# The second norm of a hybrid DiT trunk in two steps: first what feature tile 0 reads, for both groups of tokens, then the rest

## The chip, the cores and the metric

The kernel runs on one NeuronCore of a Trainium2 chip. Its engines are named as in the profile: PE (TensorE, matmuls) with PEld (its weight loads), DVE (VectorE), ACT (ScalarE), POOL (GpSimd) and SP (SyncE, which issues DMAs). The metric is the device time of one execution in microseconds (us), as the median of the runs.

## The reference

Two layers (l = 0, 1) work on 1280 tokens of 1024 features, 256 of context and 1024 of the latent. Each layer norms the tokens, projects them, runs four mixers side by side, projects the result back and adds it to x. Then comes the part that matters here:

```
x  = x + ml[2] * (y @ w_out)
h2 = rmsnorm(x, norm2) * (1 + ml[4]) + ml[3]
u, g = split(h2 @ w_up, 2)
x  = x + ml[5] * ((silu(dwconv(g)) * u) @ w_down)
```

The up-projection has 2 x 2816 columns: 22 feature tiles of 128 for u and as many for g. In layer 1 the context rows are left out.

## The kernel before

Features lie on the partitions and tokens along the free dimension, so an activation is eight tiles k = 0..7 of 128 features. Every matrix product is made of three matmuls on values split into a high part (fp32r) and a low one: hi x hi, hi x lo, lo x hi (`dense_acc`, L312 to L314). `split` (L229, L230) makes the two parts: a cast on ACT, then a subtraction on the engine that is named to it.

**The up-projection.** The latent tokens are two groups of 512: a (256 to 767) and b (768 to 1279). For feature tiles 1 to 21, `ffn_up` takes u and g of both groups at once, as a 2 x 2 block product (u or g columns times low or high features; low features times group a or b) with seven block products in place of eight. That needs combinations of the activations: B11 and B21 (low and high features of group a), T1 (low features of b less those of a), B22 (high features of b) and three more, `tops[2]`, `tops[3]` and `tops[4]`. It needs combinations of the weights too: s12, which POOL makes at L1900 and L1901 into a buffer `wr_s`, and s34, made in place at L1903 and L1904. Feature tile 0 is computed directly. Its first half uses B11 and B21; its second half, into the accumulators `pxu` and `pxg`, uses T1 and B22 alone. The accumulators of the other tiles are `px`, `py`, `pz`, and `pcu` and `pcg` for the context.

The tiles are generators. At the end of `ffn_up` they are run in this order: first half of 0, first half of 1, second half of 0, its convolution (`conv3`, ACT L729, DVE L732 and L733, L1954, L1957), second half of 1, its convolution, then the tiles 2, 3, ... one by one. L1886 loads a tile's weights through SP; L1864 copies an accumulator to the tile `u` or `gp` on ACT, L1867 adds one on DVE.

**The second norm.** Group a is normed early and its scaled values are kept in the tiles `kept` (nk in the profile). Group b comes in two pieces of 256 tokens (768 and 1024). The main program (L1766 to L1776) runs the last part of the output projection, calls `rstd_fast` for each piece (sum of squares, power on POOL, and the row `ro` copied out by ACT at L223), and then `norm_fast` (L258) for the two pieces, one after the other. For each of k = 0..3 `norm_fast` issues eight DVE instructions of 256 columns. L271 scales b12 (feature k) and b22 (feature 4 + k) and is the only one that reads x. L279 makes T1. L280 makes the input of `tops[2]`, L283 that of `tops[3]`, L288 that of `tops[4]`. L287 makes the low part of B22 (ACT makes the high part, L286). One of the splits ends on DVE (`tops[4]`); three end on POOL (T1, `tops[2]`, `tops[3]`). T1 and B22 are written to the tiles hb.

**Buffers.** `norm_fast` takes its temporaries from one tag with three buffers (L268). The pools of x (group b), of `kept` and of these temporaries are closed with `cx`, right behind the calls of `norm_fast`, and the pools w4 and u are opened next:

```
        with pool_(tc, name=f"w4{l}", bufs=3) as wq, pool_(tc, name=f"u{l}", bufs=1) as pool:
            ffn_up(K, l, act, tops, HD, (wp, wq), (ug, pool))
```

`ffn_up` takes raw weight buffers from `wp` (open since before) and `wq` (w4) by turns. The first four (u and g of tiles 0 and 1) are of `wp`; `wr_s` of tile 1 and u and g of tile 2 are of `wq`. The tile `u` of feature tile 1 is of the pool u.

**What sets the order.** The order of each engine's instructions isn't written out. A planner (the tile context, with a timeline simulation) orders them when the program is built, by their place in the source and by when its own costs let them start; a buffer is given out again when the last reader of what lay there is done. On the chip each engine then goes through its queue in that order.

Of the kernel before, what the change touches and what calls it, by code (L numbers as in the profile page):

```python
# [14 lines left out]
OP = mybir.AluOpType  # L15
# [48 lines left out]
def pool_(tc, **kw):  # L64
    return tc.tile_pool(reuse_waits="tile", **kw)


class Kern:
# [188 lines left out]
    def norm_fast(self, l, xs, rb, kept, act, tops, dsh, pool, t0, n):  # L257

        nc = self.nc
        s, d = slice(t0, t0 + n), slice(t0 - LAT[1][0], t0 - LAT[1][0] + n)
        hi, lo = act
        stt = nc.vector.scalar_tensor_tensor

        def temp(name):
            return pool.tile([P, self.nw], F32, tag="ntmp", name=f"{name}{l}1_{t0}", bufs=self.ntmps)[:, :n]

        def scaled(k):
            t = temp(f"nt{k}")  # L270
            stt(t, xs[k], self.ns[l][:, 1, k, 0:1], rb, OP.mult, OP.mult)  # L271
            return t

        for k in range(4):
            sh = self.modv[l][:, 28 + k, 0:1]
            b12, b22 = scaled(k), scaled(4 + k)
            t1, t4 = kept[k][:, d], kept[4 + k][:, d]
            t2 = temp(f"n2{k}")
            nc.vector.tensor_tensor(t1, b12, t1, OP.subtract)  # L279
            stt(t2, b22, sh, t1, OP.add, OP.subtract)  # L280
            self.split(t2, *[v[k][:, d] for v in tops[2]], nc.gpsimd)
            self.split(t1, hi[k][:, s], lo[k][:, s], nc.gpsimd)
            stt(b12, b22, dsh[:, k:k + 1], b12, OP.add, OP.subtract)  # L283
            self.split(b12, *[v[k][:, d] for v in tops[3]], nc.gpsimd)
            h = hi[4 + k][:, s]
            nc.scalar.activation(h, b22, AF.Identity, bias=sh)  # L286
            stt(lo[4 + k][:, s], b22, sh, h.bitcast(F32), OP.add, OP.subtract)  # L287
            stt(t4, t4, sh, t2, OP.add, OP.subtract)  # L288
            self.split(t4, *[v[k][:, d] for v in tops[4]], nc.vector)

# [1189 lines left out]
def trunk(ctx, tc, A, out, dbg=None):  # L1480
    nc = tc.nc
    K = Kern(ctx, tc, A, out, dbg)
# [16 lines left out]
    def open_act(name):  # L1499
        c = ExitStack()  # L1500
        ts = {}
        for q, ks in enumerate(((1, 0), (4, 5, 6, 7), (2, 3))):
            p = c.enter_context(pool_(tc, name=f"h{name}{q}", bufs=1))
            ts.update({(i, k): p.tile([P, T], F32R, name=f"h{name}{i}{k}") for k in ks for i in range(2)})
        return c, [[ts[i, k] for k in range(KT)] for i in range(2)]

    cact = act = None
    for l in range(2):
# [10 lines left out]
        if l == 0:  # L1519
# [3 lines left out]
            cact, act = open_act("a")  # L1523
        with ExitStack() as c1:
# [37 lines left out]
            if l == 0:  # L1562
                with pool_(tc, name="zs", bufs=1) as zp:
                    with pool_(tc, name="np", bufs=1) as npool:

                        xs, rb = {}, {}
# [79 lines left out]
        with ExitStack() as c3:  # L1646
            K.lo_eng = nc.gpsimd
            ep = c3.enter_context(pool_(tc, name=f"ae{l}", bufs=1))
            late = c3.enter_context(pool_(tc, name=f"al{l}", bufs=1))
# [55 lines left out]
        cact, act = open_act(f"b{l}")  # L1705
# [5 lines left out]
        def open_x(stack, order, name, **kw):  # L1711
            return {t0: stack.enter_context(pool_(tc, name=f"{name}{l}{t0}", bufs=1, **kw)).tile([P, KT, n], F32, name=f"{name}{l}{t0}") for t0, n in order}

        def resid(x, part, m):
            def evac(ps, a, n):
                c = 1 if a < TC else 0
                v = xs_(x, a, n)[:, m]
                nc.vector.scalar_tensor_tensor(v, ps, K.modv[l][:, 8 * part + m, c:c + 1], v, OP.mult, OP.add)  # L1718
            return evac

        def xs_(x, t0, n):
            b = max(q for q in x if q <= t0)
            return x[b][:, :, t0 - b:t0 - b + n]

        with ExitStack() as cx:
            x = open_x(cx, groups[-1:], "x")
            kp = cx.enter_context(pool_(tc, name=f"k2{l}", bufs=1))
            dsh = kp.tile([P, 4], F32, name=f"dsh{l}")
            nc.vector.tensor_tensor(dsh, K.modv[l][:, 28:32, 0], K.modv[l][:, 24:28, 0], OP.subtract)
            kept = []  # L1730

            def norm(t0, n, npool):
                r = K.norm_mod(l, 1, [x[t0][:, k] for k in range(KT)], act, t0, n, npool, kp if t0 == TC else None)
                if t0 == TC:
                    kept.extend(r)
                nc.scalar.dma_start(XS[:, :, t0:t0 + n], xs_(x, t0, n))

            with ExitStack() as c1:
                npool = c1.enter_context(pool_(tc, name=f"n2{l}", bufs=1))
                x.update(open_x(c1, groups[-2::-1], "x"))  # L1740
                wo = c1.enter_context(pool_(tc, name=f"wo{l}", bufs=2, side="right"))
                for k in K_ORDER:
                    for t0, n in groups:
                        raw = wo.tile([P, 512], F32, tag="yraw", name=f"yraw{l}_{k}_{t0}", bufs=4)
                        nc.sync.dma_start(raw[:, :n], YD[k][:, t0:t0 + n])
                        K.split(raw[:, :n], act[0][k][:, t0:t0 + n], act[1][k][:, t0:t0 + n], nc.vector if k % 2 else nc.gpsimd)
                    if k == 6:
                        for t0, n in groups:
                            nc.sync.dma_start(x[t0], xd[l][:, :, t0:t0 + n])
                for i, m0 in enumerate(range(0, 8, 2)):  # L1750
                    ms = range(m0, m0 + 2)
                    K.wb = (2, 4) if i % 2 else (1, 2)
                    K.dense_late([A["w_out"][l, m] for m in ms], act, K_ORDER[:-2], K_ORDER[-2:], groups[:-1], [resid(x, 2, m) for m in ms],
                                 wp if i % 2 else wo, [f"out{l}_{m}_{TC}" for m in ms])
                K.wb = (2, 4)
                for q in groups[:-1]:
                    norm(*q, npool)
            npool = cx.enter_context(pool_(tc, name=f"n3{l}", bufs=1))
            K.ntmps, K.nw = 3, 256
            ct = ExitStack()  # L1760
            tops = {q: [ct.enter_context(pool_(tc, name=f"t{q}{l}", bufs=1, side="right")).tile([P, 4, 512], F32R, name=f"top{l}{q}{i}") for i in "hl"] for q in (2, 3, 4)}
            tops = {q: [[v[:, k] for k in range(4)] for v in hl] for q, hl in tops.items()}
            ug = ct.enter_context(pool_(tc, name=f"ug{l}", bufs=1, side="right"))

            for m in range(4):
                K.dense(A["w_out"][l, m], act, KT, LAT[1:], resid(x, 2, m), wp, f"out{l}_{m}_768")  # L1766
            ws = [K.load_w(A["w_out"][l, m], KT, wp, f"out{l}_{m}_768") for m in range(4, 8)]
            late = []
            for t0, n in ((768, 256), (1024, 256)):
                for m, (hi, lo) in zip(range(4, 8), ws):  # L1770
                    ps = K.acc(f"ps_out{l}_{m}_{t0}")[:, :n]
                    K.dense_acc(ps, lambda k: hi[:, k], lambda k: lo[:, k], lambda k: act[0][k][:, t0:t0 + n], lambda k: act[1][k][:, t0:t0 + n], KT)
                    resid(x, 2, m)(ps, t0, n)
                xs = [xs_(x, t0, n)[:, k] for k in range(KT)]
                late.append((xs, K.rstd_fast(l, xs, npool, t0, n), t0, n))
                nc.scalar.dma_start(XS[:, :, t0:t0 + n], xs_(x, t0, n))  # L1776
            for xs, rb, t0, n in late:
                K.norm_fast(l, xs, rb, kept, act, tops, dsh, npool, t0, n)
        K.lo_eng = nc.gpsimd
        K.ntmps, K.nw = 2, 512  # L1780
        with pool_(tc, name=f"w4{l}", bufs=3) as wq, pool_(tc, name=f"u{l}", bufs=1) as pool:
# [32 lines left out]
        with ExitStack() as c3:  # L1814
# [4 lines left out]
            with pool_(tc, name=f"f{l}", bufs=1) as pool:  # L1819
                for i, (b0, b1) in enumerate(((0, 1), (1, 4), (4, 8), (8, 12), (12, 16), (16, 20))):  # L1820
                    with pool_(tc, name=f"e{l}{i}", bufs=1, side="right") as ep:
                        f, n = stages[i] if i < len(stages) else (None, 0)
# [9 lines left out]
            if not last:  # L1832
                cact, act = open_act(f"c{l}")
# [284 lines left out]
```

## Time and profile before

| | us |
|---|---|
| three runs | 3441.28, 3445.07, 3448.4 (median 3445.07) |
| the profiled execution | 3445.22 |
| its span | 3443.4 |
| PE busy | 3191.5 (93%) |
| DVE busy | 2128.9 (62%) |
| ACT busy | 1207.4 (35%) |
| POOL busy | 1177.6 (34%) |

The mean granted clock of TensorE is 0.963 of full speed. Times in the rows are from the start of the span. The second norm and the start of the up-projection lie at about 960 to 1040 us in layer 0 and at 2705 to 2790 us in layer 1. In a timeline a row is: start, duration, engine, line, operation, written tile <- read tiles, shape, count; in brackets how long the engine was idle before, and what released it. Rows of one kind that follow each other are merged, and their duration is that of the whole. Durations of neighbours on DVE, ACT and PE overlap, so the time that one takes in the queue is read from start to start.

### The profile page before, as it was taken

How to read it: one execution, taken by the hardware profiler on the slowest of the kernel's cores; microseconds unless marked ns; L12 is line 12 of the kernel's file. 1: busy time of each engine (PE TensorE's matmuls, PEld its weight loads, DVE VectorE, ACT ScalarE, POOL GpSimd, SP SyncE). 2: the span in 40 equal slices, each digit the busy share in tenths (PEclk: the TensorE clock that was granted, in tenths of full speed). 3: DMA queues.
4: the chain of work that ended last, by engine and by line, in shares of the span. 5: the costliest groups of instructions: out<-in, count | busy, mean ns of one | idle time of the engine just before them, and what ended most of it. 6: DMA issues, size and time to landing. Idle time of an engine off the chain costs nothing. (4 is left out here: it accounts for less than half of the span.)

```text
span 3443.4 us, 47008 instructions
## 1 busy us (share of the span) xinstructions
PE 3191.5 (93%) x17550; PEld 2644.8 (77%) x17550; DVE 2128.9 (62%) x4011; ACT 1207.4 (35%) x2013; POOL 1177.6 (34%) x1109
## 2 busy tenths in 40 slices
PE   7899997998989999998999899997998899999996
PEld 6898995664868888877788789995545788887785
DVE  7758647776484343348788583527755865556645
ACT  4223544334353333342111424533333443434211
POOL 1922424224065444442111011323332475554220
PEclk9999997999999999999999999998999999999998
DMA  5666635247222112126233565533163222223421
GB/s 204 168 198 212 175 104 159 91 145 260 94 75 80 66 66 72 62 96 198 93 104 111 146 179 173 150 114 118 52 227 102 89 92 86 74 92 128 146 68 49
DMA packets 287300, 423.53 MB, mean 123 GB/s; under 512 B 91088, under 2 KB 197344, under 8 KB 287072
## 3 DMA queue, kind: packets, MB, share of 16 engines
q1 hardware_dynamic: 176932, 301.33, 27.9%
q10 hardware_dynamic: 110140, 119.20, 10.4%
q8 instruction: 138, 2.26, 0.3%
q14 instruction: 90, 0.74, 0.1%
HBM read 301.48 MB, written 118.91 MB: 122 GB/s over the span
## 5 line engine op out<-in xcount | busy, mean ns | idle before, releaser
L312 PE MATMUL pd<-fh,wh_d 128*128 128x512 f32 (+1 forms) x896 | 328.8, 377 | 21.9 <-ACT fh L229 12.8
L313 PE MATMUL pd<-fl,wh_d 128*128 128x512 f32 (+1 forms) x896 | 333.1, 375 | 13.3 <-DVE fl L230 13.3
L314 PE MATMUL pd<-fh,wl_d 128*128 128x512 f32 (+1 forms) x896 | 329.1, 372 | 0.0
L230 POOL TENSOR_TENSOR wl_d<-wr_d,wh_d 128x1024 fp32r<-128x1024 f32 x44 | 111.3, 2549 | 467.4 <-ACT wh_d L229 458.1
L1718 DVE SCALAR_TENSOR_TENSOR xx<-pd,modv,xx 128x512 f32<-128x512 f32 (+1 forms) x248 | 164.8, 677 | 118.8 <-PE pd L314 118.4
L312 PE MATMUL ps_in<-ha,wh_in 128*128 128x384 f32 (+3 forms) x688 | 217.0, 325 | 12.0 <-ACT st L1542 11.1
L314 PE MATMUL ps_in<-ha,wl_in 128*128 128x384 f32 (+3 forms) x688 | 222.3, 323 | 0.0
L313 PE MATMUL ps_in<-ha,wh_in 128*128 128x384 f32 (+3 forms) x688 | 222.2, 323 | 0.1
L312 PE MATMUL ps_in<-hc,wh_in 128*128 128x256 f32 (+1 forms) x704 | 214.0, 306 | 5.7 <-ACT hc L244 3.7
L312 PEld LDWEIGHTS pd<-fh,wh_d 128*128 128x128 f32 x896 | 172.3, 194 | 55.5 <-ACT fh L229 15.5
L313 PE MATMUL ps_in<-hc,wh_in 128*128 128x256 f32 (+1 forms) x704 | 213.4, 304 | 0.7 <-DVE hc L245 0.7
L314 PE MATMUL ps_in<-hc,wl_in 128*128 128x256 f32 (+1 forms) x704 | 212.8, 303 | 0.0
L313 PEld LDWEIGHTS pd<-fl,wh_d 128*128 128x128 f32 x896 | 173.1, 194 | 45.5 <-DVE fl L230 18.1
L314 PEld LDWEIGHTS pd<-fh,wl_d 128*128 128x128 f32 x896 | 172.5, 193 | 28.4
L230 POOL TENSOR_TENSOR wlo_u<-wr_u,whi_u 128x1024 fp32r<-128x1024 f32 x44 | 105.7, 2402 | 217.6 <-ACT whi_u L229 195.4
L1040 ACT ACTIVATE a_E<-a_pst 128x1024 f32<-128x1024 f32 (+1 forms) x84 | 84.3, 1003 | 178.7 <-PE a_pst L1038 142.3
L229 ACT CAST wh_d<-wr_d 128x1024 fp32r<-128x1024 f32 x44 | 45.2, 1047 | 289.9 <-PE pd L313 157.2
L312 PEld LDWEIGHTS ps_in<-ha,wh_in 128*128 128x128 f32 x688 | 132.8, 194 | 14.9 <-ACT st L1542 11.8
L230 DVE TENSOR_TENSOR wlo_s<-wr_s,whi_s 128x1024 fp32r<-128x1024 f32 x42 | 70.0, 1667 | 115.3 <-ACT whi_s L229 115.3
L971 DVE TENSOR_REDUCE a_mx<-a_pm 128x1 f32<-128x512 f32 (+1 forms) x192 | 109.2, 595 | 51.3 <-PE a_pm L970 50.6
L312 PEld LDWEIGHTS ps_in<-hc,wh_in 128*128 128x128 f32 x704 | 134.4, 192 | 8.2 <-ACT hc L244 4.8
L313 PEld LDWEIGHTS ps_in<-hc,wh_in 128*128 128x128 f32 x704 | 134.8, 192 | 2.7 <-DVE hc L245 1.9
(648 smaller groups left out, 9437.5 us busy)
## 6 DMA issues: line engine op xcount, KB each, us to landing
wm<-in_w_mod SPq DMA_DIRECT2D x96, 512.0 KB
wr_in<-in_w_in SPq DMA_DIRECT2D x44, 512.0 KB
wr_u<-in_w_up SPq DMA_DIRECT2D x44, 512.0 KB
wr_g<-in_w_up SPq DMA_DIRECT2D x44, 512.0 KB
wr_d<-in_w_down SPq DMA_DIRECT2D x44, 512.0 KB
wr_out<-in_w_out SPq DMA_DIRECT2D x32, 512.0 KB
HD<-u ACTq DMA_DIRECT2D x22, 640.0 KB
hr<-HD SPq DMA_DIRECT2D x22, 640.0 KB
```

What stands on the lines that cost most here:

```text
L229: nc.scalar.copy(hi, src)
L230: (eng or nc.gpsimd).tensor_tensor(lo, src, hi.bitcast(F32), OP.subtract)
L312: mm(ps, whi(k), ahi(k), start=start and i == 0, stop=False)
L313: mm(ps, whi(k), alo(k), start=False, stop=False)
L314: mm(ps, wlo(k), ahi(k), start=False, stop=stop and i == len(ks) - 1)
L971: nc.vector.tensor_reduce(mf[:, c:c + 1] if c < 2 else mx[:, c, j:j + 1], ps[:, :kw], mybir.AxisListType.X, OP.max)
L1040: nc.scalar.activation(E[:, :, :w], ps[:, :, :w], AF.Exp, scale=scale)
L1718: nc.vector.scalar_tensor_tensor(v, ps, K.modv[l][:, 8 * part + m, c:c + 1], v, OP.mult, OP.add)
```

## The change

`norm_fast` becomes a generator with two steps. The first has, for k = 0..3, b12 and T1 with its split, then b22 and B22's two parts. The second scales b22 and b12 once more into new temporaries, and makes `tops[2]`, `tops[3]` and `tops[4]` with their splits. The main program makes a generator for each of the two pieces and runs them as first step of 768, first step of 1024, second step of 768, second step of 1024. Nothing else is touched.

```diff
--- before.py
+++ after.py
@@ -266,25 +266,32 @@
         def temp(name):
             return pool.tile([P, self.nw], F32, tag="ntmp", name=f"{name}{l}1_{t0}", bufs=self.ntmps)[:, :n]
 
-        def scaled(k):
-            t = temp(f"nt{k}")
+        def scaled(k, i):
+            t = temp(f"nt{i}{k}")
             stt(t, xs[k], self.ns[l][:, 1, k, 0:1], rb, OP.mult, OP.mult)
             return t
 
         for k in range(4):
             sh = self.modv[l][:, 28 + k, 0:1]
-            b12, b22 = scaled(k), scaled(4 + k)
-            t1, t4 = kept[k][:, d], kept[4 + k][:, d]
-            t2 = temp(f"n2{k}")
+            b12 = scaled(k, 0)
+            t1 = kept[k][:, d]
             nc.vector.tensor_tensor(t1, b12, t1, OP.subtract)
-            stt(t2, b22, sh, t1, OP.add, OP.subtract)
-            self.split(t2, *[v[k][:, d] for v in tops[2]], nc.gpsimd)
             self.split(t1, hi[k][:, s], lo[k][:, s], nc.gpsimd)
-            stt(b12, b22, dsh[:, k:k + 1], b12, OP.add, OP.subtract)
-            self.split(b12, *[v[k][:, d] for v in tops[3]], nc.gpsimd)
+            b22 = scaled(4 + k, 0)
             h = hi[4 + k][:, s]
             nc.scalar.activation(h, b22, AF.Identity, bias=sh)
             stt(lo[4 + k][:, s], b22, sh, h.bitcast(F32), OP.add, OP.subtract)
+        yield
+        for k in range(4):
+            sh = self.modv[l][:, 28 + k, 0:1]
+            t1, t4 = kept[k][:, d], kept[4 + k][:, d]
+            b22 = scaled(4 + k, 1)
+            t2 = temp(f"n2{k}")
+            stt(t2, b22, sh, t1, OP.add, OP.subtract)
+            self.split(t2, *[v[k][:, d] for v in tops[2]], nc.gpsimd)
+            b12 = scaled(k, 1)
+            stt(b12, b22, dsh[:, k:k + 1], b12, OP.add, OP.subtract)
+            self.split(b12, *[v[k][:, d] for v in tops[3]], nc.gpsimd)
             stt(t4, t4, sh, t2, OP.add, OP.subtract)
             self.split(t4, *[v[k][:, d] for v in tops[4]], nc.vector)
 
@@ -1774,8 +1781,9 @@
                 xs = [xs_(x, t0, n)[:, k] for k in range(KT)]
                 late.append((xs, K.rstd_fast(l, xs, npool, t0, n), t0, n))
                 nc.scalar.dma_start(XS[:, :, t0:t0 + n], xs_(x, t0, n))
-            for xs, rb, t0, n in late:
-                K.norm_fast(l, xs, rb, kept, act, tops, dsh, npool, t0, n)
+            fast = [K.norm_fast(l, xs, rb, kept, act, tops, dsh, npool, t0, n) for xs, rb, t0, n in late]
+            for f in fast + fast:
+                next(f, None)
         K.lo_eng = nc.gpsimd
         K.ntmps, K.nw = 2, 512
         with pool_(tc, name=f"w4{l}", bufs=3) as wq, pool_(tc, name=f"u{l}", bufs=1) as pool:
```

## Rows read from the trace of the kernel before

**Rows 1.** Three stretches: us, PE, PEld, DVE, ACT, POOL busy, TensorE clock, DMA share.
```profile
984.00:1012.45 28.45, 16.06 (x49) 10.56 (x49) 25.22 (x42) 13.60 (x30) 19.20 (x20) 0.76 0.11 37
2725.50:2755.91 30.41, 16.88 (x49) 11.08 (x49) 27.01 (x45) 14.28 (x32) 20.21 (x21) 0.72 0.10 35
1062.00:1500.00 438.00, 438.00 (x2311) 375.71 (x2310) 167.61 (x158) 164.19 (x210) 196.85 (x103) 1.00 0.19 67
```

**Rows 2.** Waits of PE over the run: us in total, times, longest us.
```profile
PE pxu L312 <- ACT hb L229: 25.6, 8, 7.4
```

**Rows 3.** Timeline of PE, layer 0: start us, us, line, operation.
```profile
983.68 0.28 PE L314 MATMUL pcu<-hb,wlo_u 128*128 128x256 f32 x1
...
1003.69 0.80 PE L312 MATMUL pxu<-hb,whi_u 128*128 128x512 f32 x1 [2.17 <-ACT hb L229]
...
1004.71 0.63 PE L313 MATMUL pxu<-hb,whi_u 128*128 128x512 f32 x1
1005.13 0.63 PE L314 MATMUL pxu<-hb,wlo_u 128*128 128x512 f32 x1
...
1012.22 0.39 PE L314 MATMUL pxg<-hb,wlo_g 128*128 128x512 f32 x1
1012.45 0.40 PE L312 MATMUL px<-top02h,whi_s 128*128 128x512 f32 x1
```

**Rows 4.** Timeline of DVE, layer 0, around the second norm.
```profile
969.23 0.88 DVE L271 SCALAR_TENSOR_TENSOR nt<-x,ns,ro 128x256 f32<-128x256 f32 x2 [1.53 <-ACT ro L223]
...
1001.93 0.87 DVE L271 SCALAR_TENSOR_TENSOR nt<-x,ns,ro 128x256 f32<-128x256 f32 x2
1002.72 0.41 DVE L279 TENSOR_TENSOR nk<-nt,nk 128x256 f32<-128x256 f32 x1
1003.05 0.41 DVE L230 TENSOR_TENSOR top04l<-nk,top04h 128x256 fp32r<-128x256 f32 x1
1003.39 0.47 DVE L280 SCALAR_TENSOR_TENSOR n<-nt,modv,nk 128x256 f32<-128x256 f32 x1
1003.78 0.95 DVE L283 SCALAR_TENSOR_TENSOR nt<-nt,dsh,nt 128x256 f32<-128x256 f32 x1
1004.66 0.95 DVE L287 SCALAR_TENSOR_TENSOR hb<-nt,modv,hb 128x256 fp32r<-128x256 f32 x1
...
1006.95 0.95 DVE L230 TENSOR_TENSOR top04l<-nk,top04h 128x256 fp32r<-128x256 f32 x1 [0.47 <-ACT top04h L229]
...
1016.42 3.31 DVE L732 SCALAR_TENSOR_TENSOR cv<-gp,vec,cv 128x1281 f32<-128x1281 f32 x1 [0.30 <-ACT cv L729]
```

**Rows 5.** Groups of DVE's instructions from 969 to 1008 us: busy us, mean ns.
```profile
L271 DVE SCALAR_TENSOR_TENSOR nt<-x,ns,ro 128x256 f32<-128x256 f32 x16 | 9.0, 587 | 1.6 <-ACT ro L223 1.5
```

**Rows 6.** Timeline of POOL, layer 0.
```profile
1003.71 0.74 POOL L230 TENSOR_TENSOR hb<-nk,hb 128x256 fp32r<-128x256 f32 x1 [1.99 <-ACT hb L229]
...
1006.16 1.46 POOL L1900 TENSOR_TENSOR wr_s<-wr_g 128x512 f32<-128x512 f32 x1
```

**Rows 7.** Timeline of SP, layer 0.
```profile
1002.82 0.33 SPq L1886 DMA_DIRECT2D wr_u<-in_w_up  x1
```

**Rows 8.** Timeline of ACT, layer 0.
```profile
1007.99 0.59 ACT L1864 COPY u<-px 128x512 f32<-128x512 f32 x1 [1.07 <-DVE top04l L230]
...
1009.09 1.05 ACT L229 CAST whi_s<-wr_s 128x1024 fp32r<-128x1024 f32 x1 [0.23 <-POOL wr_s L1901]
```

**Rows 9.** Timeline of DVE, layer 1.
```profile
2713.04 0.88 DVE L271 SCALAR_TENSOR_TENSOR nt<-x,ns,ro 128x256 f32<-128x256 f32 x2
...
2745.25 0.87 DVE L271 SCALAR_TENSOR_TENSOR nt<-x,ns,ro 128x256 f32<-128x256 f32 x2
```

**Rows 10.** Timeline of SP, layer 1.
```profile
2746.14 0.33 SPq L1886 DMA_DIRECT2D wr_u<-in_w_up  x1
```

**Rows 11.** Timeline of ACT, layer 1.
```profile
2751.32 0.59 ACT L1864 COPY u<-px 128x512 f32<-128x512 f32 x1 [1.07 <-DVE top14l L230]
```

**Rows 12.** Timeline of PE, layer 1.
```profile
2755.91 0.40 PE L312 MATMUL px<-top12h,whi_s 128*128 128x512 f32 x1
```

## The prediction

> **What bounds the kernel now.** I began with the stretches around the two second norms [rows 1]. [...] In the stretch of each layer between the last work that doesn't need the second group and the first matmul of feature 1's second half, TensorE runs only 49 matmuls in 28.45 us (layer 0) and 30.41 us (layer 1), at a mean clock of 0.76 and 0.72. 48 of these belong to feature 0 (T1 and B22, four k, three products, for u and for g). At the spacing of 0.23 us that two full-clock neighbours show [rows 3] they need 11.0 us, so the stretches lose 17.4 and 19.4 us.
>
> The table of waits names the loss: feature 0's `pxu` waits eight times, 25.6 us in all, for the cast of `hb` [rows 2]; the rest is half clock, where neighbours are 0.42 us apart [rows 3]. The casts come late because of VectorE's chain. The timeline of DVE shows it in one piece from 969.23 to 1007.90 (1006.95 + 0.95) in layer 0 [rows 4], from 2713.04 [rows 9] to about 2751.2, where ACT is let go, in layer 1 [rows 11]. By the code that is 64 instructions (eight per k, four k, two groups). Alone, the scalar-tensor-tensor form takes 0.395 us (two in 0.79) and the plain tensor-tensor 0.33; beside POOL's splits it is 0.88 [rows 4].
>
> Then I asked what waits for the **end** of the chain, since feature 0 needs only half of it. SP issues the first weight load of feature 2 at 1002.82 [rows 7], 0.02 us after the pair of L271 that is the last to read x ends (1002.80) [rows 4]; in layer 1 it is 2746.14 [rows 10] after 2746.12 [rows 9]. The code says why: the pools of x, kept and n3 close just ahead of w4 and u, whose buffers take their place. Feature 1's `wr_s`, made by POOL at L1900, is the first buffer of w4. ACT's copy into `u` of feature 1 waits for the last `top` split (1007.99 in layer 0, 2751.32 in layer 1) [rows 8, 11], and the `tops` themselves are read only from feature 1 on. So TensorE can do feature 0 without step two, and nothing after it.
>
> **Part by part, per layer.** *Moved:* the combinations T1 and B22 of both groups come first. Step one issues four DVE instructions, two ACT casts and one POOL split per k. Eight of these cost 8 x (3 x 0.395 + 0.33) = 12.1 us, and 8 splits. A split costs DVE about 0.88 - 0.395 = 0.48 us [rows 4], so 3.9 us more: 16 us from 969.23, which is 985, or up to 3 us later with the evacuations that stand between (the remainder below). TensorE runs dry at 983.7 + 0.28 [rows 3]; by then three of the four k are there, and feature 0 ends at about 984 + 11.0 = 995, with little or no stall. That part does what it is for.
>
> *Added:* b12 and b22 are scaled twice, 16 more L271 beside the 16 there now [rows 5]. No DMA and no semaphore of SP is added, and POOL has the same 24 splits. The check on the prices is the chain of now: 48 x 0.395 + 16 x 0.33 + 24 x 0.48 = 35.8 us of the 38.7; two evacuations and a wait of 0.47 [rows 4] are in the remaining 2.9. DVE is full there, so nothing hides the 16: 16 x 0.395 = **6.3 us**, and the chain ends at 1014.2 and 2757.5. From below, 16 x 0.33 = 5.3; from above, each meets a split, 16 x 0.88 = 14.1. I take 6.3, since the splits are no more than before. [...]
>
> *The release of x* moves further than the end. Its last reader now has seven instructions behind it; in the change there are three (b12's subtraction, t4, t4's split): 2 x 0.395 + 0.33, two splits and the wait of 0.47, or 2.5 us. So x is let go at 1014.2 - 2.5 = 1011.7, which is **8.9 us later** than 1002.80, and 2755.0 in layer 1. SP's load of feature 2's u weights stands there, and the g weights behind it in SP's queue.
>
> *What TensorE then waits for:* `whi_s` of feature 1. POOL began L1900 at 1006.16 [rows 6], 3.36 us after the release, because three splits were ahead of it (the first at 1003.71) [rows 6]. In the change none to two are ahead: 0 to 2.3 us, I take 1.2. From L1900 to the end of ACT's cast is 1009.09 + 1.05 - 1006.16 = 3.98 us [rows 6, 8]. So 1011.7 + 1.2 + 4.0 = 1016.9. The copy into `u` (1014.2 + 0.1 + 0.6) [rows 8] is there before it; the copy stands at the head of ACT's queue until then, ahead of that cast.
>
> *The clock:* TensorE idles in one piece from 995 to 1016.9. After a gap it now runs at 0.42 us per matmul, from 1003.69 on [rows 3]. Nine matmuls at 0.42 in place of 0.23 are 1.7 us; the bounds are 0 and 3.
>
> *Sum:* feature 1's second half begins at 1012.45 now [rows 3] and 2755.91 in layer 1 [rows 12]. In the change it is 1016.9 + 1.7 - 1012.45 = +6.2 us, and 2755.0 + 1.2 + 4.0 + 1.7 - 2755.91 = +6.0 us. Behind it TensorE is full [rows 1], so both reach the end: +12.2 us. Against the profiled execution's 3445.2 us (span 3443.4), which is 0.15 above the median of the runs, that is **3457 us**. The stall isn't removed: it goes from `pxu` (four short gaps) to `px` of feature 1 (one gap of 22 us). The release is 2.6 us more late than the chain's end, so with the low bounds (5.3 + 2.6) a layer is 1002.8 + 7.9 + 0 + 4.0 - 1012.45 = +2.3 us, and with the high ones (14.1 + 2.6) 1002.8 + 16.7 + 2.3 + 4.0 + 3 - 1012.45 = +16.4.
>
> **Rivals.** A measurement of this kernel can tell 0.2%, 6.9 us, from no change.
>
> *No difference that can be told.* The low bounds hold: the planner puts L1900 at once behind x's release, and the clock costs nothing. +2 to +3.4 us a layer: about 3450 us. For it speaks that POOL has gaps of 2 us already now [rows 6]; against it that 6.3 us of full DVE have no cover. Chance 0.25.
>
> *Faster.* POOL's splits, with one instead of three per k in step one, run beside DVE instead of blocking it. The 24 x 0.48 = 11.5 us vanish, the chain ends at 1002.7, x is let go 1.6 us ahead of that (two splits less), and feature 1 begins at 1001.1 + 1.2 + 4.0 + 1.7 = 1008.0, 4.4 us earlier per layer: about 3436 us. It decides once the chain grows by less than about 0.1 us (6.3 - 6.2). The most that any form of this can give is 17.4 + 19.4 = 36.8 us, 3408 us. Against it: in these rows two-input DVE instructions are at 0.88 whenever a split runs. [...] By that rule, with which 0.88 against 0.395 agrees, I give it 0.10.
>
> *Slower still.* Feature 0's convolution is ready at 995, 17 us earlier than now, and its buffer is free at the chain's end. If it gets ahead of the DVE split of `whi_s`, its first pass alone costs 3.31 us [rows 4] per layer: about 3464 us, within the slower side. Chance 0.12 of the 0.65.
>
> *It doesn't do what it says.* The planner, not the source, orders each queue. If it fills DVE with step-two work ahead of the second group's step one, `pxu` still waits, but the chain's end, and so the time, is that of the forecast.
>
> **Numbers.** Slower by over 0.2%: 0.65, the forecast with its late form; within: 0.25; faster: 0.10. The range from 3441 to 3470 takes in the forecast, most of the no-difference case and the late form; outside are the faster case and the high bounds.
>
> **What would show it.** Right: L271 x64 over the run; `pxu`'s 25.6 us of waits nearly gone; a wait of some 20 us per layer in front of feature 1's `px`; SP's load at about 1011.7 and 2755.0; ACT's copy into `u` near 1014.3 and 2757.6. Wrong: that load within 4 us of where it is now, a DVE chain that ends before 1010, or matmuls of feature 1 between 996 and 1012.

## The result and the profile after

The changed kernel took 3461.99 us (median of 3461.51, 3461.53, 3462.45 and 3466.82), the kernel before 3446.74 us (median of four runs beside it): the difference of the medians is 15 us. The ratio on record is 1.0052, 95% interval 1.0037 to 1.0067 (the quotient of these two medians is 1.0044). It is slower. The profiled execution took 3461.51 us with a span of 3459.6 us, 16.2 us over that of before.

The table of waits of TensorE (us in total, times, longest) shows the exchange. The eight waits of `pxu` [rows 2] are gone but for one of 0.3 us in layer 1, and two long ones stand at its head, one per layer:

```profile
PE px L319 <- ACT whi_s L229: 46.8, 2, 24.6
...
PE px L319 <- ACT u L1872: 2.6, 2, 2.4
```

DVE's instructions L271 over the run (busy us, mean ns) are doubled, 64 in place of 32:

```profile
L271 DVE SCALAR_TENSOR_TENSOR nt<-x,ns,ro 128x256 f32<-128x256 f32 x64 | 33.0, 536 | 1.7 <-ACT ro L223 1.6
```

The timeline of PE (start us, us, line, operation, idle before), layer 0 first. It begins with the first product of feature 0 that uses the second half of the weights' rows (`pyu`), which I use as a mark, and ends with the first of the down-projection (`pd`); the last three rows are of layer 1:

```profile
956.60 0.47 PE L319 MATMUL pyu<-hb,whi_u 128*128 128x512 f32 x1
...
996.22 0.39 PE L321 MATMUL pxg<-hb,wlo_g 128*128 128x512 f32 x1
1018.87 0.79 PE L319 MATMUL px<-top02h,whi_s 128*128 128x512 f32 x1 [22.27 <-ACT whi_s L229]
...
1021.60 0.63 PE L319 MATMUL py<-hb,whi_u 128*128 128x512 f32 x1
1022.03 0.54 PE L320 MATMUL py<-hb,whi_u 128*128 128x512 f32 x1
1022.40 0.40 PE L321 MATMUL px<-top02h,wlo_s 128*128 128x512 f32 x1
...
1029.43 0.38 PE L321 MATMUL pcg<-hb,wlo_g 128*128 128x256 f32 x1 [1.08 <-POOL wlo_g L230]
...
1032.93 0.79 PE L319 MATMUL px<-top03h,whi_s 128*128 128x512 f32 x1 [2.40 <-ACT u L1872]
...
1041.40 0.40 PE L319 MATMUL px<-top04h,whi_g 128*128 128x512 f32 x1
...
1546.55 1.36 PE L319 MATMUL pd<-fh,wh_d 128*128 128x256 f32 x4 [1.73 <-ACT fh L229]
...
2767.33 0.79 PE L319 MATMUL px<-top12h,whi_s 128*128 128x512 f32 x1 [24.58 <-ACT whi_s L229]
...
2773.43 0.39 PE L321 MATMUL px<-top12h,wlo_s 128*128 128x512 f32 x1
```

Feature 0's second half is done at 996.6, at full clock (granted 1.00) and without a stall; before it ended at 1012.6 [rows 3]. Then TensorE has nothing for 22.27 us. Feature 1 goes on 6.42 us later than before [rows 3] (1.5 us of this came ahead of the norm), runs at 0.43 us per matmul until 1022.4 (granted 0.50), and then stalls twice more, for 3.5 us, where the kernel before had no such wait. Layer 1 differs: behind the wait of 24.58 us come fourteen matmuls at the half clock (granted 0.50, 0.43 us apart), until 2773.43, and then no stall.

What stood in the way, on the other engines, first DVE:

```profile
970.97 1.28 DVE L271 SCALAR_TENSOR_TENSOR nt<-x,ns,ro 128x256 f32<-128x256 f32 x3 [1.55 <-ACT ro L223]
...
1012.20 0.47 DVE L271 SCALAR_TENSOR_TENSOR nt<-x,ns,ro 128x256 f32<-128x256 f32 x1
...
1013.86 0.41 DVE L230 TENSOR_TENSOR top04l<-nk,top04h 128x256 fp32r<-128x256 f32 x1
...
1016.61 2.48 DVE L739 SCALAR_TENSOR_TENSOR cv<-gp,vec,cv 128x1281 f32<-128x1281 f32 x1 [0.99 <-ACT cv L736]
1019.02 2.30 DVE L230 TENSOR_TENSOR wlo_s<-wr_s,whi_s 128x1024 fp32r<-128x1024 f32 x1
1021.24 2.56 DVE L740 SCALAR_TENSOR_TENSOR cv<-gp,vec,cv 128x1281 f32<-128x1281 f32 x1
1023.72 3.43 DVE L230 TENSOR_TENSOR wlo_s<-wr_u,whi_s 128x1024 fp32r<-128x1024 f32 x1
1027.10 4.79 DVE L1965 TENSOR_TENSOR u<-u,cv 128x256 f32<-128x256 f32 x2
```

then SP, POOL and ACT:

```profile
1012.70 0.33 SPq L1894 DMA_DIRECT2D wr_u<-in_w_up  x1
```

```profile
1014.45 0.73 POOL L230 TENSOR_TENSOR top03l<-nt,top03h 128x256 fp32r<-128x256 f32 x1 [0.80 <-ACT top03h L229]
1015.14 1.27 POOL L1908 TENSOR_TENSOR wr_s<-wr_g 128x512 f32<-128x512 f32 x1
1016.48 1.26 POOL L1909 TENSOR_TENSOR wr_s<-wr_s,wr_u 128x512 f32<-128x512 f32 x1
```

```profile
1014.30 0.59 ACT L1872 COPY u<-px 128x512 f32<-128x512 f32 x1
...
1017.78 1.04 ACT L229 CAST whi_s<-wr_s 128x1024 fp32r<-128x1024 f32 x1 [1.20 <-POOL wr_s L1909]
...
1031.92 0.33 ACTq L1967 DMA_DIRECT2D HD<-u  x1
1032.29 0.58 ACT L1872 COPY u<-px 128x512 f32<-128x512 f32 x1 [5.22 <-DVE u L1965]
```

The last reader of x ends at 1012.67, SP's load follows at 1012.70 (before: 1002.82 [rows 7]), and behind it come POOL's sums, the cast, TensorE. POOL's sums don't start at x's release: two splits of step two stand ahead of them in POOL's queue, the last at 1014.45, so the sums begin 2.44 us behind the load. The kernel before had room on this path: the cast of `whi_s` ended at 1010.14 [rows 8], and TensorE, busy without a gap from 1003.69 on, came to it 2.3 us later. A second thing is to be seen: the convolution of feature 0 (L739, L740, L1965) now stands ahead of feature 1's splits (`wlo_s`) and between them, while in the kernel before its first pass came at 1016.42 [rows 4], behind both. ACT's queue then holds the store of feature 0 until L1965 is done, and behind it the copy of `px` that TensorE waits for at 1032.93.

**One table for all runs.** Single executions differ by some us ahead of the norm (the first `pyu` came at 955.1, as shown here, and at 953.0 us in two executions of the kernel before).

```profile
955.12 0.47 PE L312 MATMUL pyu<-hb,whi_u 128*128 128x512 f32 x1
```

So I read each layer from the first `pyu` to the first `pd`, in three parts: up to feature 1's second half (first `px` from `top02h` or `top12h`; "restart"), from there to the first `px` from `top04h` or `top14h`, and the whole. All are differences of start times in the timeline of PE, in us, layer 0 / layer 1. The mixer column lies between the up-projections, in layer 1's mixer, which no edit touches: first `a_pkn` to first `a_pr`. It is no measure of equal work: 619 matmuls lie between its marks in the kernel before, 600 in the second execution of the changed kernel, where 19 (of `pm`, `a_pst`, `a_po` and `m_pf`) lie outside them. The whole way between the layers, from the first `pd` of layer 0 to the first `pyu` of layer 1, has 6224 matmuls in both: 1172.8 and 1176.0 us in the two executions of the kernel before, 1166.1 and 1168.7 us in those of the changed one.

| kernel | restart | to `top4` | whole | mixer | time, ratio to before (95%) |
|---|---|---|---|---|---|
| before | 57.3 / 48.1 | 16.7 / 17.3 | 579.9 / 450.9 | 139.5 | |
| before again | 57.3 / 48.1 | 16.7 / 17.3 | 580.0 / 450.9 | 139.4 | 3446.33 (one run) |
| changed | 62.3 / 54.6 | 22.5 / 20.2 | 589.9 / 461.0 | 133.2 | 1.0052 (1.0037 to 1.0067) |
| changed again | 62.0 / 54.6 | 22.6 / 19.0 | 589.8 / 460.2 | 132.5 | 1.0047 (1.0034 to 1.0060) |
| scalings alone | 63.3 / 54.6 | 18.1 / 18.0 | 587.4 / 460.6 | 136.4 | 1.0048 (1.0036 to 1.0060) |
| order alone | 57.5 / 47.3 | 21.2 / 20.0 | 584.4 / 455.7 | 139.2 | 1.0040 (1.0028 to 1.0053) |

The whole repeats within 0.1 us in layer 0 and 0.8 us in layer 1. The change costs 10.0 + 10.1 = 20.1 us there. In the profiled executions 1.5 us more came ahead of the norm and 1.2 us at the end; 6.6 us were regained between the layers: 20.1 + 1.5 + 1.2 - 6.6 = 16.2, the difference of the spans.

### The profile page after: what moved, and what is told of

Read it like the earlier page. It is cut to its first block, busy times and chain, and to the rows that moved or that the text cites. A ratio compares the mean times of both kernels' runs of the same rounds, so it can differ in the third digit from the quotient of the medians.

```text
span 3459.6 us, 47004 instructions
## 1 busy us (share of the span) xinstructions
PE 3180.6 (92%) x17521; PEld 2640.4 (76%) x17550; DVE 2144.6 (62%) x4043; ACT 1206.0 (35%) x2013; POOL 1196.1 (35%) x1109
## 5 line engine op out<-in xcount | busy, mean ns | idle before, releaser
L319 PE MATMUL ps_in<-ha,wh_in 128*128 128x384 f32 (+3 forms) x688 | 217.4, 326 | 17.6 <-ACT st L1549 17.2
```

The lines of the kernel that those rows point to most:

```text
L319: mm(ps, whi(k), ahi(k), start=start and i == 0, stop=False)
```

## The experiments

Theory A: the sixteen extra scalings lengthen DVE's chain, and x, with it `whi_s`, comes late. Theory B: the order itself costs, whatever the number of instructions.

**Again, unaltered: the changed kernel and the kernel before.**

> The changed kernel again, unaltered, for the parts of its time that lie outside the two stretches. If they come from the order of the instructions, they repeat within 0.3 us: the first scaling of layer 0 at 971.0, that of layer 1 at 2717.9, the last store of a feature tile at 1565.1 and 3192.8. If they are chance of one execution, the starts differ by some us, while the lengths within the stretches (43.3 us from the first scaling of layer 0 to the end of its last split, 22.3 us of idle TensorE ahead of the second tile) repeat.

> The kernel before again, unaltered, for the parts of its time outside the two stretches. From the first product of pxu to the first of pd it took 564.5 us in layer 0 and 444.6 us in layer 1, between the layers 1179.1 us. If the 4 to 7 us by which the changed kernel was shorter between the layers (1172.5 and 1175.0 us) are chance, this run shows another value between 1172 and 1180; if they are of the changed kernel's order, it repeats 1179 within 1 us. The two stretches repeat within 1 us either way.

The changed kernel took 3460.62 us. The starts moved (first scaling at 968.66 and 2718.29), so they are chance; the stretches repeated, as the table shows, and so did the chain (43.3 us) and the idle time (22.30 us). The kernel before took 3446.33 us, and its stretches repeated too. Between them, from the first `pd` to the first `pxu`, it took 1182.4 us: 3.3 us more than 1179.1, which is neither of the two cases expected. Executions of one kernel differ there by about 3 us, so what the changed kernel gains between the layers is 4 to 10 us.

The stretch in the mixer repeats, 139.5 and 139.4 against 133.2 and 132.5. These are its marks, the kernel before first, then the changed kernel:

```profile
2362.87 0.62 PE L312 MATMUL a_pkn<-a_kvh,a_wkh 128*64 128x432 f32 x1
...
2502.38 1.08 PE L1004 MATMUL a_pr<-a_S,ones 128*64 128x512 f32 x4
```

```profile
2374.10 0.62 PE L319 MATMUL a_pkn<-a_kvh,a_wkh 128*64 128x432 f32 x1
...
2507.35 1.08 PE L1011 MATMUL a_pr<-a_S,ones 128*64 128x512 f32 x4
```

The code there is the same, but the planner writes TensorE's queue in another order for the changed kernel, and since 19 matmuls now lie outside the marks, the 6 to 7 us are not all gain. That the order is the cause of the gain between the layers was not tried.

**Scalings alone.** The kernel before, one step, with b12 and b22 scaled a second time (the input of `tops[3]` and its split thereby move behind the two parts of B22):

```diff
-            stt(b12, b22, dsh[:, k:k + 1], b12, OP.add, OP.subtract)
-            self.split(b12, *[v[k][:, d] for v in tops[3]], nc.gpsimd)
 ...
+            b22, b12 = scaled(4 + k, 1), scaled(k, 1)
+            stt(b12, b22, dsh[:, k:k + 1], b12, OP.add, OP.subtract)
+            self.split(b12, *[v[k][:, d] for v in tops[3]], nc.gpsimd)
```

> The kernel before, in its one step and its order, with the sixteen extra scalings per layer alone added: before the sum for tops[3] both halves are scaled a second time. Theory A (length of the chain): slower by about what the change costs, two layers of 6.3 us and what the clock adds, 3446 to about 3459 (3456 to 3462), and TensorE's second feature tile starts about 6 us later in each layer. Theory B (the order costs): within 0.2% of the kernel before, 3440 to 3453.

3463.13 us, ratio 1.0048, a little above A's range. The restart is 6.0 and 6.5 us later than before, as A said; from there to `top4` the time grows by only 1.4 and 0.7 us, and in layer 1 another 2.5 us come further on. Sixteen instructions per layer, nearly in the old order, cost 7.5 and 9.7 us of whole stretch, against 10.0 and 10.1 for the change.

But the loss doesn't come by the path that A names. Here TensorE still waits for `hb` in feature 0 (eight waits, 31.8 us in place of 25.6 [rows 2]) and does the rest of feature 0 partly at the half clock (0.43 us from matmul to matmul up to 1012.45); in layer 0 it comes to `px` without a wait, 0.8 us after the cast of `whi_s` is done. PE, then ACT:

```profile
1007.42 0.80 PE L313 MATMUL pxu<-hb,whi_u 128*128 128x512 f32 x1 [1.76 <-ACT hb L229]
...
1017.00 0.40 PE L313 MATMUL px<-top02h,whi_s 128*128 128x512 f32 x1
```

```profile
1015.15 1.05 ACT L229 CAST whi_s<-wr_s 128x1024 fp32r<-128x1024 f32 x1 [1.34 <-POOL wr_s L1902]
```

So this run shows what a longer chain costs TensorE, not that x's release carries it.

**In place.** The changed kernel with the scaled values written over x and read there by step two:

```diff
 ...
-            t = temp(f"nt{i}{k}")
-            stt(t, xs[k], self.ns[l][:, 1, k, 0:1], rb, OP.mult, OP.mult)
-            return t
+            stt(xs[k], xs[k], self.ns[l][:, 1, k, 0:1], rb, OP.mult, OP.mult)
+            return xs[k]
 ...
```

> The changed kernel, with one thing undone: the scaled values of the first step are written over x, and the second step reads them there, so the sixteen extra scalings per layer (L271 of the changed kernel) are gone, while the two steps and their order stay. Theory A (the length of the chain decides: sixteen scalings at 0.395 us delay the release of x, and with it POOL's first sum, ACT's cast of whi_s and TensorE's second feature tile): the last reader of x comes 6.3 us earlier in each layer (layer 0: the load behind it at 1006.4 instead of 1012.7 us), TensorE resumes about 6 us earlier, and the time falls by about 12.5 us, from 3462 to about 3449. Theory B (the order costs, not the number of instructions: the first tile's convolution gets ahead of the splits, the clock drops in the gap): the chain is shorter but the time stays at 3457 or above.

3451.55 us, ratio 1.0023 (1.0014 to 1.0032), whole stretches 584.0 and 451.1. This looks like A, but the timeline of DVE shows that it isn't a clean test: `t2` of the first group (L289) runs ahead of the second group's scalings (L270 x8), so the two-step order was not kept, and TensorE has stalls in feature 0 again.

```profile
980.15 0.96 DVE L289 SCALAR_TENSOR_TENSOR n<-x,modv,nk 128x256 f32<-128x256 f32 x1
...
985.66 3.73 DVE L270 SCALAR_TENSOR_TENSOR x<-x,ns,ro 128x256 f32<-128x256 f32 x8
```

**Order alone.** The same, with step two of both groups tied to the end of step one:

```diff
 ...
+            _, q = [next(f) for f in fast]
+            for g, v in zip(gate, (K.modv[l][:, 28:32, 0], dsh)):
+                nc.vector.scalar_tensor_tensor(g, q, 0.0, v, OP.mult, OP.add)
 ...
```

where q is a few columns of the last value of step one, and step two takes its shifts from `gate`.

> The two-step order alone: values scaled in place in x (no extra scalings), and the second step of both groups tied to the end of the second group's first step by one small operation, so that the order is the changed kernel's, which the first run in place did not keep (there the first group's second step ran ahead of the second group's first). Theory A (the sixteen scalings carry the cost): from the first product of pyu to the first of pd 6.3 us less per layer than in the changed kernel: 589.8 to about 583.5 and 460.6 to about 454, the time 3461 to about 3449. Theory B (the order itself costs): within 3 us of the changed kernel's stretches, 587 and 458 or more, the time 3455 or above.

The stretches are 584.4 and 455.7, within 2 us of A's numbers (583.5 and 454), 5.5 and 5.3 us below the changed kernel; the waits for `whi_s`, 22.27 and 24.58 us there, are 15.90 and 14.44 us. This is the comparison that bears on A in the two-step order. (Step two reads x itself here, so x's last reader isn't a scaling.) But the stretches are 4.5 and 4.8 us above the kernel before: B holds for that part. The restart is where it was (+0.2 and -0.8 us); the loss comes after it. PE in layer 0 and, in front of the second wait, ACT:

```profile
1014.65 0.80 PE L318 MATMUL px<-top02h,whi_s 128*128 128x512 f32 x1 [15.90 <-ACT whi_s L229]
...
1028.91 0.50 PE L318 MATMUL px<-top03h,whi_s 128*128 128x512 f32 x1 [3.17 <-ACT u L1875]
```

```profile
1027.91 0.33 ACTq L1970 DMA_DIRECT2D HD<-u  x1
1028.28 0.58 ACT L1875 COPY u<-px 128x512 f32<-128x512 f32 x1 [4.98 <-DVE u L1968]
```

In layer 0 it is the convolution of feature 0, early because feature 0 is early, that gets between feature 1's steps. In layer 1 the 2.7 us up to `top4` are matmuls at the half clock behind the restart (0.43 us apart) and one wait of 0.67 us for `wlo_s`; 2.9 us come further on, of which only a wait of 1.00 us has a name.

The two parts don't add up to the change: scalings alone and order alone cost 7.5 + 4.5 = 12.0 us in layer 0 and 9.7 + 4.8 = 14.5 us in layer 1, the change 10.0 and 10.1. With the scalings paid, the two-step order adds some 2.5 us in layer 0 and next to nothing in layer 1; they overlap, and no run divides the cost between them.

The time, 3460.52 us, is no lower than the changed kernel's, though the stretches are 10.8 us shorter in sum; the way between the layers is back at 1175.2 us, 9 us more than in the changed kernel's profiled execution. (Against the runs of the kernel before that stood beside each, order alone is 13.2 us slower and the changed kernel again 15.6.) By its stretches the run is A's, by its time B's; totals of two versions can't be compared below some 7 us here, the stretches can.

**The store of feature 0 on SP's queue**, in the changed kernel:

```diff
-        nc.scalar.dma_start(HD[j][:, h0:], u[:, h0:])
+        (nc.scalar if j else nc.sync).dma_start(HD[j][:, h0:], u[:, h0:])
```

> The changed kernel, with the store of the first feature tile's result (L1967) issued by SyncE instead of ScalarE, for this tile alone. In the changed kernel's layer 0 ScalarE stands 5.22 us in front of this store, behind it lies the copy of u from PSUM for which TensorE then waits 2.40 us. Theory C (the convolution of the first tile, which now gets ahead of the second tile's splits, costs a part of its own through this queue): the wait of 2.40 us in layer 0 is gone, with the half clock behind it 3 to 4 us, and the time falls from 3462 to about 3458. Theory A (only the later release matters): the wait moves to another place, and the time stays within 2 us of 3462.

3459.55 us, ratio 1.0044 (1.0032 to 1.0056). In layer 0 the wait of 2.40 us is gone and the whole falls to 588.0, but in its place come waits of 1.11 us (for a copy of `gp`) and 0.73 us (for an addition to it); in layer 1, which had no such wait, it rises to 462.2. The store stands among SP's loads of weights there, but the next load behind it comes as late as without it (15.2 us after the first), so why layer 1 grows stays open. The time lies between the two forecasts. The queue of ACT carries 1.8 us in layer 0, not 3 to 4, and this is no cure.

**Fill the gap.** Feature 1 computed directly, from B11, B21, T1 and B22 as feature 0 is, but with B11's products made a second time for group b: 120 products of 512 columns in place of 84, and no sums of weights and no `tops`. The core of the edit (the turn of the weight buffers is shifted with it):

```diff
+        if j == 1:
+            u1, g1 = bank(K.pd, "pu"), bank(K.pb, "pg")
+            prod(u1, uw, 0, B11, True)
+            prod(u1, uw, 4, B21, False)
 ...
+            for w, db, p in ((uw, ub, K.pd), (gw, gb, K.pb)):
+                x = bank(p, "pz")
+                prod(x, w, 0, B11, True)
+                prod(x, w, 0, T1, False)
+                prod(x, w, 4, B22, False)
```

> The kernel before, with its norm in one step, but the second feature tile computed directly as the first is (B11, B21, T1, B22: 120 products with 512 columns instead of 84), so that it needs neither sums of weights nor tops and can lie in the gap in which TensorE waits for the norm. Theory A (the price of the change is the gap of TensorE that grows with the chain): whoever fills the gap gets it back; the 36 extra products cost 36 x 0.23 = 8.3 us per layer, the gap of some 17 us to 20 us per layer is filled, so about 8 us per layer less than before: 3445 to about 3429 (3424 to 3436). Theory D (something else than TensorE's work sets the pace in these stretches: the queue of DVE or POOL work behind the norm): no gain or a loss, 3445 to 3462.

> The changed kernel (two steps, sixteen extra scalings per layer) with the same direct second feature tile. Theory A: the chain's length no longer decides, since the third tile needs the chain's end only some 33 us after the first tile's second half; the sixteen scalings are hidden, and the time is within 4 us of the run with one step (about 3429). Theory B (the two steps or their scalings cost by themselves): 8 us or more above that run.

> The two steps with the scaled values kept in x (no extra scalings) and the direct second feature tile. Theory A: as the other two with the direct tile, within 4 us of them (about 3429): none of the three has a gap that the chain sets. Theory B: the shorter chain shows, 8 us or more below the changed kernel with the direct tile.

| kernel | whole | time | ratio to before (95%) |
|---|---|---|---|
| before, direct | 575.7 / 448.4 | 3446.09 | 0.9996 (0.9988 to 1.0005) |
| changed, direct | 580.4 / 450.2 | 3452.78 | 1.0022 (1.0011 to 1.0034) |
| in place, direct | 580.5 / 452.1 | 3452.99 | 1.0029 (1.0017 to 1.0041) |

What A says of the change is borne out: with work for the gap, the changed kernel's stretches come down by 9.5 and 10.8 us, to those of before, and its 22 us wait is gone. Between the changed kernel and the one-step kernel 4.7 and 1.8 us remain (6.7 us in the time), more than the 4 us in all that A allowed and less than B's 8. The kernel in place is no faster than the changed one (580.5 and 452.1 against 580.4 and 450.2), but it doesn't keep the two-step order, as above, so it isn't a test of the scalings by themselves. What A says of a gain isn't borne out: 4.2 and 2.5 us less than before where 8 were expected, and nothing in the time, which is what D forecast. The 36 extra products cost an estimated 36 x 0.23 = 8.3 us a layer, and new waits follow, now in feature 2 (changed kernel, direct):

```profile
1033.64 0.50 PE L319 MATMUL px<-top02h,whi_s 128*128 128x512 f32 x1 [3.15 <-ACT u L1872]
...
1045.82 0.70 PE L319 MATMUL px<-top03h,whi_s 128*128 128x512 f32 x1 [4.82 <-ACT u L1872]
```

**Cut the path behind x.** Feature 1's sum `s12` in a free slot of the lo weights, so that POOL's sums need not wait for x (the turn of the weight buffers is shifted here too):

```diff
-            s12 = raw("s")
+            s12 = raw("s") if j > 1 else wps[0].tile([P, KT, P], F32, tag="wlo", name=f"wr_s{nm}", bufs=4)
```

> The kernel before, with the sum of weights of the second feature tile (s12) put in a free slot of the lo weights, not in the buffer that lies over x: the path from the last reader of x over POOL's sums and ACT's cast to TensorE is cut, the norm is unchanged. Theory A (this path holds TensorE from 1005 to 1012 us in layer 0 of the kernel before): some 7 us less per layer, the stretches 580.0 and 450.9 down to about 573 and 444, the time 3445 to about 3431. Theory E (POOL's sums, now early, lie among the norm's splits on POOL and lock DVE out, so the chain grows by what is gained): within 2 us per layer of before, 3441 to 3449.

> The changed kernel with the same early sum of weights. Theory A (the change is paid over the release of x, POOL's sums and the cast behind it, while TensorE has nothing that it could do in the gap): TensorE takes the parts of the second tile that need only the first step (z and the context, 8.4 us) into the gap and goes on at the chain's end, not 4.6 us after it: 13 us less per layer, the stretches 589.8 and 460.6 down to about 577 and 448, the time 3461 to about 3436. Theory B (the length of the chain alone decides, the path behind it does not): 4 us less per layer at most, 3453 or above.

> The order alone (no extra scalings, tied) with the early sum of weights. Theory A: what was taken from the changed kernel adds up, 6.3 us for the scalings and 13 us for the path, so the stretches come to about 571 and 442 and the time to about 3426, below both kernels, and about 5 us below the kernel before with the early sums, since the two-step order gives TensorE work that the one-step order does not. Theory E (POOL's early sums lengthen the chain): at or above the kernel before with the early sums.

| kernel | restart | to `top4` | whole | time | ratio to before (95%) |
|---|---|---|---|---|---|
| before, early sums | 64.2 / 52.2 | 14.8 / 15.9 | 584.2 / 455.3 | 3457.98 | 1.0035 (1.0022 to 1.0048) |
| changed, early sums | 70.5 / 56.6 | 17.6 / 19.4 | 591.0 / 461.6 | 3462.96 | 1.0050 (1.0037 to 1.0064) |
| order alone, early sums | 63.6 / 50.2 | 18.2 / 19.7 | 583.7 / 455.6 | 3454.37 | 1.0026 (1.0014 to 1.0038) |

All three miss A, by 11 to 14 us a layer. A's premise for the first run doesn't hold either: in the kernel before TensorE was at work on feature 0 until 1012.45, and `whi_s` was there 2.3 us earlier. The second run lies where B put it, but since its chain comes later it doesn't show B. The third is within 0.5 us of the first in both layers, so the two-step order gains nothing even here. The growth that E names is what happened, and it cost more than E said: 4.2 and 4.4 us over the kernel before in the first run. The sums did go early, and there they met the norm. POOL and DVE of the first of them, layer 0:

```profile
962.47 1.45 POOL L1900 TENSOR_TENSOR wr_s<-wr_g 128x512 f32<-128x512 f32 x1
964.00 1.36 POOL L1901 TENSOR_TENSOR wr_s<-wr_s,wr_u 128x512 f32<-128x512 f32 x1
965.44 1.35 POOL L1903 TENSOR_TENSOR wr_u<-wr_u,wr_g 128x512 f32<-128x512 f32 x1
966.75 1.45 POOL L1904 TENSOR_TENSOR wr_u<-wr_u,wr_s 128x512 f32<-128x512 f32 x1
```

```profile
964.52 5.01 DVE L212 TENSOR_TENSOR sb_n<-sb_n,sq_n 128x256 f32<-128x256 f32 x5
...
978.50 0.88 DVE L271 SCALAR_TENSOR_TENSOR nt<-x,ns,ro 128x256 f32<-128x256 f32 x2 [3.49 <-ACT ro L223]
```

The chain begins 978.50 - 958.44 (its first `pyu`) = 20.1 us behind `pyu`, where it was 14.1 in the kernel before (969.23 [rows 4] - 955.1). That POOL locks DVE out is E's supposition; the rows show 1.00 us for each of the five additions, where the kernel before has 0.51. The path from x's release to `whi_s` is cut, and the chain itself comes 6 us later; the five additions account for 2.5 us of these, the rest isn't divided up. So whether that path alone could be shortened stays open; no place for the sums was found that doesn't touch the norm. No version beat the kernel before.

## Why the prediction was right, step by step

Predicted 3457.0 us with 3441 to 3470, slower at 0.65; measured 3461.99 and 15 us slower. The exchange that was forecast is what the trace shows: feature 0 early, one long wait ahead of feature 1, paid by a longer chain. Its sum, +12.2, was 3 to 4 us low, and that it came so near is in part luck: the two stretches cost 20.1 us, 8 more than forecast, and 6.6 us came back between the layers, which the forecast did not have.

- *Moved.* Feature 0 would end at about 995 with little or no stall: 996.6, none in layer 0.
- *Added.* 6.3 us for sixteen L271, chain end at 1014.2: it ended at 1014.27 (1013.86 + 0.41), but it had begun 1.74 us later, so its length is 43.3 us in place of 45.0. It grew by 4.6 us in layer 0 (from 38.7), under even the low bound of 5.3, and by 5.6 in layer 1 (38.2 to 43.8), not by 6.3; that it ended where forecast is luck. In one step the same scalings moved the restart by 6.0 and 6.5 us, by waits for `hb` and half clock.
- *Release of x.* Predicted 8.9 us later than before: counted from the first `pyu`, (1012.70 - 956.6) - (1002.82 - 955.1) = 8.4 us. SP's load stood at 1012.70 for 1011.7, and ACT's copy into `u` at 1014.30 for "near 1014.3".
- *POOL and the cast.* 1.2 + 4.0 us from the release to the end of the cast; it took 6.1 in layer 0 (1012.70 to 1018.82) and 7.2 in layer 1 (2760.10 to 2767.27). In both layers two splits stood ahead of L1908, which began 2.44 us behind the load, just over my upper bound of 2.3. Restart predicted 4.5 us later, measured 4.9; in layer 1 predicted 4.3, measured 6.5. There POOL's second sum took 2.32 us besides, where it took 1.36 in the kernel before, with the convolution's first pass on DVE beside it:

```profile
2762.54 1.27 POOL L1908 TENSOR_TENSOR wr_s<-wr_g 128x512 f32<-128x512 f32 x1
2763.88 2.32 POOL L1909 TENSOR_TENSOR wr_s<-wr_s,wr_u 128x512 f32<-128x512 f32 x1
```

- *The clock.* 1.7 us, from nine matmuls. In layer 0 the rows show eight steps of about 0.43 in place of 0.23, 1.6 us, and about as much again after the wait at 1032.93, which I hadn't foreseen. In layer 1 fourteen steps take 6.1 us in place of 3.2: 2.9 us, which is all that layer 1 loses between restart and `top4`, and just within the upper bound of 3 (1.7 us in the second execution).
- *The term that was missing* is, in layer 0, the order's own cost. "Behind it TensorE is full" was read from rows that begin at 1062 us [rows 1], behind the place where the changed kernel stalls again for 3.5 us. I had the convolution that gets ahead as a rival with 3.31 us per layer and a chance of 0.12, as something beside the forecast; in layer 0 it is a part of it. The run with the order alone, with no scaling added and no later restart, lost 4.5 and 4.8 us, clock and waits together, of which the forecast had the clock's 1.7. The rival's direction was right, its place only in part: besides the first pass, the store behind it in ACT's queue held TensorE. In layer 1 of the changed kernel there is no such stall; its surplus is POOL's later and longer sums, the longer half clock and 0.8 us further on.
- *What was not foreseen the other way* is the way between the layers, 4 to 10 us shorter with the changed kernel's order of instructions. Without it the change would have cost some 20 us. Its cause stays open.
- *The rivals.* Faster: by POOL's splits beside DVE. Nothing of the kind; the chain grew. No run shows the rule by which the prediction gives this 0.10; the rows show 0.88 us beside a split and 0.395 alone [rows 4]. No difference: this asked for low bounds in all terms. "It doesn't do what it says" happened to the run in place, not to the change.

## What to carry to other kernels

A norm split in two so that TensorE gets its first half early bought nothing here, with the scalings or without them: the stall moves to the next consumer, and the instructions that the split repeats on a full engine lengthen it. Before such a change ask what TensorE could do in the new gap, and what the work that becomes ready early (here a convolution and a store in a shared queue) will get ahead of. Judge a change of some us by a stretch between two marks that repeats, and count the instructions between them, since a planner can move work across a mark. The total alone doesn't do: here it moved by as much in a part of the kernel that no edit touched.

## What the runs showed of the hardware that was not expected

DVE's additions took twice as long beside POOL's additions of 128x512, far from the place that I had looked at. In the kernel before, five DVE additions of 128x256 in the sum of squares take 2.53 us:

```profile
960.55 2.53 DVE L212 TENSOR_TENSOR sb_n<-sb_n,sq_n 128x256 f32<-128x256 f32 x5
```

With POOL's sums beside them for most of the time the same five took 5.01 us (above), 1.00 us each and not 0.51. It goes both ways, and in the two pairs that I read the one that began second was drawn out. In layer 0 of the changed kernel POOL's second sum began at 1016.48 and took 1.26 us, and DVE's pass of 1281 columns, begun 0.13 us later, took 2.48 us (1.94 ns a column). In layer 1 DVE began first, at 2763.80, and took 1.29 us for 1024 columns (1.26 ns a column); POOL's sum, 0.08 us later, took 2.32 us:

```profile
2763.80 1.29 DVE L739 SCALAR_TENSOR_TENSOR cv<-gp,vec,cv 128x1024 f32<-128x1024 f32 x1 [0.78 <-ACT cv L736]
```
